# A two-layer attention decoder in split f32: four heads per attention unit on a fixed beat, the projection's last tiles by halves, residual loads for the MLP issued earlier

## The chip, the core and the metric

One core of one Trainium2 chip runs the whole program. The metric is the device time of one execution in microseconds (us). A core has a matrix engine (TensorE, PE in the tables; its loads of stationary operands are listed apart as PEld), VectorE (DVE), ScalarE (ACT), GpSimd (POOL) and SyncE (SP), which here only issues DMAs. Each engine runs its own instructions in order and waits on semaphores that the others raise.

## The reference

The kernel computes two layers of a decoder on a sequence of 1024 tokens with 1024 channels, all in f32:

```python
hn = rmsnorm(h, norm1[i])
# hn @ w_in: 256 pool columns, then q, k, v of 12 heads of 64
# 3 groups of 4 heads, (window, dilation) = (128,1), (512,4), (2048,16)
s = jnp.einsum('brnqhd,brnkhd->brnhqk', qs, kb) * (HEAD_DIM ** -0.5)
s = jnp.where(valid, s, -jnp.inf)
e = jnp.exp(s - jnp.max(s, axis=-1, keepdims=True))
o = jnp.einsum('brnqhk,brnkhd->brnqhd', e / l, vb)     # l: sum of e
# outputs of the three groups weighed by softmax of their log-sum-exps
h = h + concat(pool mixer, attention) @ w_out
# then rmsnorm, a squared-ReLU MLP of width 4096 and its residual add,
# then a gated per-layer embedding; after both layers a last rmsnorm
```

A block is 128 queries of one group. It sees one or two blocks of 128 keys.

## The kernel before

**How products are made.** An f32 operand is split into a high and a low part that the matrix engine takes at full speed (type fp32r), and a product is three matmuls: high by high, high by low, low by high. Activations lie transposed, 128 channels by 1024 tokens in a buffer. `products_by_row` (L570) makes several outputs at once, one row of the operand after another. The MLP's up and down products use a scheme of seven products per 2x2 block of tiles (class Seven): the pieces of a step are called P1 to P7 and run in the order P1, P7, P6, P2, P5, P4, P3, in groups of matmuls whose outputs are called X, Y and Z in the traces. For it, activations (`xP`, `wP`) and weights (`u0p`, `u1p` for up, `d0p`, `d1p` for down) are combined and split ahead: ScalarE writes the high part (L330 for weights), VectorE the low part (L332), GpSimd makes the weights' sums (`u0s`, L311 to L318).

**What sets the order.** The order of instructions is written by hand through a clock object `ck`. Each matmul of a large product advances it by a modelled time (`ck.tick(225.0)`), and generators that were started with `ck.go` are resumed when the modelled time that they asked for has come: their instructions then land between the large matmuls. `ck.need` and `ck.waiting` hold an instruction back until the one that writes its operand has been written down. So small matmuls of attention lie among the 128x512 matmuls of the input projection (`in` in the rows) and of the output projection (`po`).

**Buffers.** One SBUF pool has 49 buffers of equal size (`blk`). A buffer that the program drops is given to the next request, and its new writer waits until the last reader is through. PSUM banks come from four tags: `mm` (3 banks), `s` (2), `e` (2), `o` (1).

**Attention.** `attend` (L833) starts one generator `unit` (L763 to L831) per block and, in groups 0 and 1, per pair of heads, spaced by 3400 of modelled ns; group 2 has one unit for all four heads, every 2500. A unit writes down: the scores `s` (L783); per head a masked copy with the row maximum on VectorE (L789), a scaled maximum `nm` (L793), and the exponentials on ScalarE (L796); then the transposes `e` through the identity (L805), a copy of them to SBUF (`et`, L810 or L812), the products with v (`o`, L819) and the copies of these (L825, L828).

**End of the projection.** The output projection has eight tiles of 128 channels, each of two halves of 512 tokens. Tiles 0 to 5 go one half after another (L1122 to L1132). Tiles 6 and 7 are made together: four outputs in banks `mm`, `o`, `e`, `e`, interleaved by rows of the operand, and all four end with the last row:

```python
        outs = [(bank(f"po{L}", ("mm", "o", "e", "e")[k]), wk(ws[k % 2], range(8)), hs(k // 2)) for k in range(4)]
        products_by_row(outs, catl)
        ck.go(last_evac([o[0] for o in outs]))
```

`products_by_row` drops row i of the operand (`cat`, a high and a low buffer for each of the eight rows) when its products are written down. `last_evac` (L1070) then adds the residual to both halves (L1079 from PSUM, L1081) and starts the splits for the MLP (`xpiece`, L1040 to L1046); `combine` (L1094 to L1114) makes further pieces. The MLP's first group of matmuls (X, Y, Z, L566) follows at once.

**Residual in the MLP.** The residual was stored to memory as `h_d`. In the down products each piece's result is added to an accumulator `acc` (L1242), whose tiles are loaded from `h_d` (L1290) when piece P1 of a step is written down. SyncE also issues the loads of the activations' pieces (`wP` from `x_d`, L1226), their stores (L1199 to L1216) and the loads of weights (`d0r`, L284).

Of the kernel before, what the change touches and what calls it, by code (L numbers as in the profile page):

```python
# [9 lines left out]
F32 = mybir.dt.float32  # L10
# [106 lines left out]
def body(nc, tc, pools, A, out):  # L117
    sb, small, ps, dr = pools
    ck = Clock()
# [501 lines left out]
    def layer(L, hT, norm, tabs):  # L621
# [141 lines left out]
        def unit(g, n, ps_, q, k, vget, o, lag):  # L763

            two = (n > 0) if g == 0 else (n % 2 == 1) if g == 1 else False
            nb = 2 if two else 1
            np_ = len(ps_)
            K = 128 * nb
            if g == 2:
                mk = cst[:, C_MASK[2]:C_MASK[2] + 128]  # L770
            else:
                mk = cst[:, C_MASK[g] + 256 - K:C_MASK[g] + 256]
            heads = [(i, hh, 2 * p + hh) for i, p in enumerate(ps_) for hh in range(2)]
            for p in ps_:
                for t in (q[p], k[p]):
                    for hf in range(2):
                        ck.need((id(t), hf))
            sp = [bank(f"s{g}", "s", (128, np_, K)) for _ in range(2)]
            k0 = (n - nb + 1) * 128
            for i, hh, h in heads:  # L780
                r = slice(64 * hh, 64 * hh + 64)
                p = ps_[i]
                nc.tensor.matmul(sp[hh][:, i], q[p][r, n * 128:n * 128 + 128],  # L783
                                 k[p][r, k0:k0 + K], start=True, stop=True)
            ck.now += 218.0 * nb * np_
            yield 350.0
            sm = blk(f"sm{g}", F32, (128, np_, 2, K))
            for i, hh, h in heads:
                nc.vector.tensor_tensor_reduce(sm[:, i, hh], sp[hh][:, i], mk, 1.0, -3.0e38,  # L789
                                               OP.add, OP.max, ml[g][:, n, h:h + 1])  # L790
            nm = small.tile([128, 2 * np_], F32, name="nm", tag="nm", bufs=6)
            h0 = 2 * ps_[0]
            nc.vector.tensor_scalar(nm, ml[g][:, n, h0:h0 + 2 * np_], -0.125, None, op0=OP.mult)  # L793
            yield 500.0 + 300.0 * nb * np_
            for j, (i, hh, h) in enumerate(heads):
                nc.scalar.activation(sm[:, i, hh], sm[:, i, hh], AF.Exp, bias=nm[:, j:j + 1],  # L796
                                     scale=0.125, accum_out=ml[g][:, n, 4 + h:5 + h])
            yield 900.0 * np_ + 300.0
            if ps_[-1] == 1:
                stats_out(g, n)  # L800
            stats[g] += np_
            ep = bank(f"e{g}", "e", (128, np_, 2, nb, 128))
            for i, hh, h in heads:
                for kb in range(nb):
                    nc.tensor.transpose(ep[:, i, hh, kb], sm[:, i, hh, kb * 128:kb * 128 + 128], ident)  # L805
            ck.now += 107.0 * 2 * nb * np_
            yield 300.0
            et = blk(f"et{g}", F32, (128, np_, 2, nb, 128))
            if (n + ps_[0]) % 2:
                nc.vector.tensor_copy(et, ep)  # L810
            else:
                nc.scalar.activation(et, ep, AF.Copy)  # L812
            yield 900.0 + lag
            while not all(vok(g, n, p) for p in ps_):
                yield 500.0
            op = bank(f"o{g}", "o", (128, np_, 128))
            for i, hh, h in heads:
                for kb in range(nb):
                    nc.tensor.matmul(op[64 * hh:64 * hh + 64, i], vget(n - nb + 1 + kb, h),  # L819
                                     et[:, i, hh, kb], start=kb == 0, stop=kb == nb - 1)  # L820
            ck.now += 107.0 * 2 * nb * np_
            yield 300.0
            for i, p in enumerate(ps_):
                if g == 0:
                    nc.scalar.activation(o[p].rearrange("p (r n a) -> p n r a", r=8, n=8)[:, n],  # L825
                                         op[:, i].rearrange("p (r a) -> p r a", r=8), AF.Copy)
                elif g == 1:
                    nc.scalar.activation(o[p].rearrange("p (s x a) -> p x s a", s=2, x=8)[:, n],  # L828
                                         op[:, i].rearrange("p (s a) -> p s a", s=2), AF.Copy)
                else:  # L830
                    nc.scalar.activation(o[p][:, n * 128:n * 128 + 128], op[:, i], AF.Copy)  # L831

        def attend(g, q, k, vget, base, gap, lag=0.0):  # L833
            o = [blk(f"o{g}{p}_{L}") for p in range(2)]
            oT[g] = o
            i = 0
            for n in range(8):
                for ps_ in (((0, 1),) if g == 2 else ((0,), (1,))):
                    ck.go(unit(g, n, ps_, q, k, vget, o, lag), ("o", g, n, ps_[-1]), base + gap * i)
                    i += 1  # L840

        for g in range(2):
# [4 lines left out]
                   5000.0, 3400.0)  # L847
# [4 lines left out]
               3500.0, 2500.0)  # L852
# [121 lines left out]
        def weigh(g, p, hf):  # L974
            i = 2 * g + p
            keys = {("wb", g, p)}
            for n in range(4 * hf, 4 * hf + 4) if g == 2 else range(8):
                keys.add(("o", g, n, 1 if g == 2 else p))
# [91 lines left out]
        def last_evac(ps_):  # L1070
            add = nc.vector.tensor_tensor
            halves = []
            for k in (0, 1):
                res[6 + k] = blk(f"res{6 + k}_{L}")
            for hf in range(2):
                for m in (6, 7):
                    a = res[m][:, hs(hf)]
                    halves.append(a)
                    add(a, ps_[2 * hf + m - 6], f(hT[m][0][:, hs(hf)]), op=OP.add)  # L1079
                for m in (6, 7):  # L1080
                    add(res[m][:, hs(hf)], res[m][:, hs(hf)], f(hT[m][1][:, hs(hf)]), op=OP.add)  # L1081
                    P = {(6, 0): "P1", (7, 0): "P2", (7, 1): "P3"}.get((m, hf))
                    if P:
                        g = gt[:, G_N2 + 8 * L + m:G_N2 + 8 * L + m + 1]
                        ck.go(xpiece(3, P, res[m][:, hs(hf)], g, 2600.0 if P == "P3" else 900.0))
                yield 2800.0
# [4 lines left out]
            for k, a in enumerate(halves):  # L1091
                yield from norm2.add(a, k // 2)
# [440 lines left out]
```

## Time and profile before

| | us |
|---|---|
| median of 3 runs | 2332.04 (2331.57 to 2335.32) |
| the profiled execution, whole | 2332.01 |
| its span, first to last instruction | 2330.2 |
| PE busy | 2280.8 (98%) |
| DVE, ACT, POOL busy | 1677.5, 1014.7, 694.3 |

The rows below are of four kinds: the page's table of engines; the waits of one engine, added up by line and by what ended them; timelines, which list the instructions of an engine in a stretch with their start and their duration, and in brackets the idle time before them with what ended it; and a table of stretches with the granted clock. Layer 1 runs from the start to about 1150 us, layer 2 after it. Durations in a timeline overlap: a matmul's row reaches from its start to its modelled end, so what a matmul costs is read from one start to the next.

### The profile page before, as it was taken

What the parts mean: (1) busy time and instruction counts of PE and PEld (TensorE: products, weight loads), DVE (VectorE), ACT (ScalarE), POOL (GpSimd) and SP (SyncE); (2) the same over time, 40 slices, a digit from 0 to 9 for tenths busy, and PEclk for the clock granted to TensorE, in tenths of its full rate; (3) what the DMA queues carried; (4) which work ended last, traced back from release to release, by engine and by line L of the source; (5) the groups of instructions that cost most, each with busy time, mean ns of one, the idle gap of its engine ahead of it and who ended that gap; (6) DMA issues with size and microseconds to landing.
All of it is one profiled execution on the core that took longest, in us unless ns stands there. A gap on an engine that the chain in (4) does not pass through costs nothing.

```text
span 2330.2 us, 30901 instructions
## 1 busy us (share of the span) xinstructions
PE 2280.8 (98%) x11088; PEld 1841.8 (79%) x11088; DVE 1677.5 (72%) x2832; ACT 1014.7 (44%) x2147; POOL 694.3 (30%) x538
## 2 busy tenths in 40 slices
PE   8999999999999999999999999999999999999998
PEld 6767788788887788888887767878888877888888
DVE  7555677787778787886565467688777787787845
ACT  5243543433345444354324345434333443434645
POOL 5111136333332232342221122354333323333322
PEclk9999999999999999999999999999999999999999
DMA  5011133254447745432220111433444575545214
GB/s 181 19 38 28 38 92 109 77 171 153 155 150 257 234 136 164 148 95 70 61 59 19 38 38 39 106 112 117 155 156 157 198 237 179 172 127 169 89 55 136
DMA packets 296369, 275.65 MB, mean 118 GB/s; under 512 B 12476, under 2 KB 224056, under 8 KB 296216
## 3 DMA queue, kind: packets, MB, share of 16 engines
q1 hardware_dynamic: 293624, 270.04, 37.3%
q0 software_dynamic: 2272, 3.61, 0.9%
q8 instruction: 87, 1.43, 0.3%
q14 instruction: 66, 0.54, 0.1%
q10 hardware_dynamic: 320, 0.03, 0.0%
HBM read 200.99 MB, written 72.58 MB: 117 GB/s over the span
## 4 chain that ended last, share of the span: by engine, by line
PE 82%; DVE 8%; DMA 3%; POOL 2%; ACT 2%; issue 2%; SPq 0%; DVEq 0%; ACTq 0%; POOLq 0%
PE X L566 27%; PE Z L566 12%; PE Y L566 7%; PE in L551 6%; PE in L549 6%; PE in L553 5%; PE gt L553 2%; PE gt L551 2%; PE gt L549 2%; PE s L783 2%; PE o L819 2%; DVE wP L1230 2%; DMA wP<-x_d 2%; PE e L805 1%; POOL res L1058 1%
## 5 line engine op out<-in xcount | busy, mean ns | idle before, releaser
L1230 DVE TENSOR_TENSOR wP<-wP 128x512 fp32r<-128x512 f32 x252 | 197.5, 808 | 0.9 <-ACT wP L1228 0.9
L566 PE MATMUL X<-wP,d1p 128*128 128x512 f32 x768 | 186.2, 395 | 10.2 <-DVE acc L1242 9.7
L566 PE MATMUL X<-wP,d0p 128*128 128x512 f32 x768 | 186.2, 395 | 10.0 <-DVE acc L1242 9.5
L566 PE MATMUL X<-xP,u0p 128*128 128x512 f32 x768 | 183.2, 391 | 0.4 <-ACT y L1164 0.4
L566 PE MATMUL X<-xP,u1p 128*128 128x512 f32 x768 | 183.1, 391 | 0.4 <-ACT y L1164 0.4
L566 PEld LDWEIGHTS X<-wP,d0p 128*128 128x128 f32 x768 | 145.5, 191 | 44.4 <-DVE acc L1242 6.9
L566 PEld LDWEIGHTS X<-wP,d1p 128*128 128x128 f32 x768 | 145.4, 190 | 44.6 <-DVE acc L1242 7.2
L566 PEld LDWEIGHTS X<-xP,u0p 128*128 128x128 f32 x768 | 144.6, 189 | 30.9 <-ACT y L1164 0.8
L566 PEld LDWEIGHTS X<-xP,u1p 128*128 128x128 f32 x768 | 144.6, 189 | 30.9 <-ACT y L1164 0.8
L1190 ACT ACTIVATE y<-y 128x1024 f32<-128x1024 f32 x64 | 67.5, 1055 | 211.8 <-DVE y L1187 211.8
L1228 ACT ACTIVATE wP<-wP 128x512 fp32r<-128x512 f32 x252 | 147.3, 617 | 24.6 <-DMA wP<-x_d 22.2
L190 DVE SCALAR_TENSOR_TENSOR wl<-wr,gt,wh 128x128 fp32r<-128x128 f32 (+1 forms) x288 | 119.9, 447 | 38.5 <-ACT wh L196 38.3
L678 POOL TENSOR_TENSOR rot<-rot,s 128x512 f32<-128x512 f32 x48 | 61.4, 1284 | 278.6 <-DVE rot L676 217.6
L1242 DVE TENSOR_TENSOR acc<-acc,X 128x512 f32<-128x512 f32 x128 | 87.4, 683 | 77.9 <-PE X L566 63.8
L796 ACT ACTIVATE sm<-sm,nm 128x128 f32<-128x128 f32 (+1 forms) x192 | 84.5, 442 | 93.3 <-DVE nm L793 93.1
L196 ACT ACTIVATE wh<-wr,gt 128x128 fp32r<-128x128 f32 (+1 forms) x304 | 104.3, 396 | 0.5 <-DMA wr<-in_w_in_dram 0.5
L566 PE MATMUL Z<-xP,u0p 128*128 128x512 f32 x384 | 93.5, 393 | 4.6 <-DVE res L1079 4.6
L566 PE MATMUL Z<-xP,u1p 128*128 128x512 f32 x384 | 93.5, 393 | 4.5 <-DVE res L1079 4.5
L789 DVE CUSTOM_DVE_ANT_0 sm<-s,cst 128x128 f32<-128x128 f32 (+1 forms) x192 | 58.3, 347 | 52.1 <-PE s L783 52.0
L566 PE MATMUL Z<-wP,d0p 128*128 128x512 f32 x384 | 91.9, 389 | 0.0
L566 PE MATMUL Z<-wP,d1p 128*128 128x512 f32 x384 | 91.9, 389 | 0.0
L330 ACT ACTIVATE d0p<-d0s 128x512 fp32r<-128x512 f32 x64 | 40.1, 628 | 111.9 <-PE X L566 65.7
(474 smaller groups left out, 5923.8 us busy)
## 6 DMA issues: line engine op xcount, KB each, us to landing
wP<-x_d SPq DMA_DIRECT2D x252, 256.0 KB, 3.6
x_d<-ys SPq DMA_DIRECT2D x64, 512.0 KB, 3.6
wr<-in_w_in_dram SPq DMA_DIRECT2D x40, 512.0 KB, 4.2
u0r<-in_w_up_dram SPq DMA_DIRECT2D x32, 512.0 KB, 5.1
x_d<-y SPq DMA_DIRECT2D x32, 512.0 KB, 2.8
u1r<-in_w_up_dram SPq DMA_DIRECT2D x32, 512.0 KB, 5.4
d0r<-in_w_down_dram SPq DMA_DIRECT2D x28, 512.0 KB, 5.8
d1r<-in_w_down_dram SPq DMA_DIRECT2D x28, 512.0 KB, 5.9
```

What stands on the lines that cost most here:

```text
L190: nc.vector.scalar_tensor_tensor(l[:, k], raw[:, k], gs[k], f(h[:, k]), op0=OP.mult, op1=OP.subtract)
L196: nc.scalar.activation(h[:, k], raw[:, k], AF.Copy, scale=gs[k])
L549: nc.tensor.matmul(p, wh, h[:, cols], start=first and i == 0, stop=False)
L551: nc.tensor.matmul(p, wh, l[:, cols], start=False, stop=False)
L553: nc.tensor.matmul(p, wl, h[:, cols], start=False, stop=last and i == n - 1)
L566: nc.tensor.matmul(p, w[:, a, i], x[:, b], start=first and i == 0 and a == b == 0, stop=i == n - 1 and a == 1, skip_group_check=not first)
L678: nc.gpsimd.tensor_tensor(a, a, tb["s"][:, hs(hf)], op=OP.mult)
L796: nc.scalar.activation(sm[:, i, hh], sm[:, i, hh], AF.Exp, bias=nm[:, j:j + 1], scale=0.125, accum_out=ml[g][:, n, 4 + h:5 + h])
L1190: nc.scalar.activation(y, y, AF.Square)
L1228: nc.scalar.activation(t[:, 0], f(t[:, 1]), AF.Copy)
L1230: nc.vector.tensor_tensor(t[:, 1], f(t[:, 1]), f(t[:, 0]), op=OP.subtract)
L1242: nc.vector.tensor_tensor(a, a, p, op=OP.add)
```

## The change

Three parts. **Attention:** `unit` becomes a class `Unit` with all four heads of a block in every group. In groups 0 and 1 one generator `beats` writes down, every 5900 of modelled ns, the transposes of the block before, the products with v of the block before that and the scores of the current block, one behind another with no large matmul between. In group 2 the beat stays 2500 and the transposes come two beats after the scores. The four `nm` become one operation per block, and the copies of the transposes of a two-key-block unit are split over VectorE and ScalarE. **Projection:** tiles 6 and 7 are made for the first half of the tokens, in the two banks `e`, and then for the second half, in `mm` and `o`; `last_evac` is called after each; rows of `cat` are dropped in the second pass only. **Residual loads:** the tiles of step 0 are asked for five pieces ahead of the end of the up products, those of step k+1 at piece P4 of step k.

```diff
-    def products_by_row(outs, rhs, first=0, n=8):
+    def products_by_row(outs, rhs, n=8, last=True):
...
-            rhs[i] = None
+            if last:
+                rhs[i] = None
...
+            def beats():
+                t = ck.now
+                for i in range(8 + 2 * late):
+                    if 0 <= i - late < 8:
+                        u = units[i - late]
+                        u.turn()
+                        if g == 2:
+                            ck.go(alone(u))
+                    if g < 2 and i >= 2 * late:
+                        u = units[i - 2 * late]
+                        while not (vok(g, u.n, 0) and vok(g, u.n, 1)):
+                            yield 500.0
+                        u.mix()
+                    if i < 8:
+                        units[i].scores()
+                    t += gap
+                    yield max(100.0, t - ck.now)
...
             attend(g, q, k, lambda n, h, v=v: v[h // 2][:, n, 64 * (h % 2):64 * (h % 2) + 64],
-                   5000.0, 3400.0)
+                   5000.0, 5900.0, 1)
...
-               3500.0, 2500.0)
+               3500.0, 2500.0, 2)
...
-        outs = [(bank(f"po{L}", ("mm", "o", "e", "e")[k]), wk(ws[k % 2], range(8)), hs(k // 2)) for k in range(4)]
         cat.clear()
-        products_by_row(outs, catl)
-        ck.go(last_evac([o[0] for o in outs]))
+        for hf in range(2):
+            outs = [(bank(f"po{L}", ("e", ("mm", "o")[m])[hf]), wk(ws[m], range(8)), hs(hf)) for m in range(2)]
+            products_by_row(outs, catl, last=hf == 1)
+            ck.go(last_evac([o[0] for o in outs], hf))
...
+        def acc_load(t):
+            for m in (2 * t, 2 * t + 1):
+                acc[m] = blk(f"acc{m}_{L}")
+                nc.sync.dma_start(out=acc[m], in_=h_d[m])
...
+            if q == len(seq) - 5:
+                acc_load(0)
...
+            if P == "P4" and k < 3:
+                acc_load(k + 1)
             if P == "P1":
-                for m in (2 * t, 2 * t + 1):
-                    if acc[m] is None:
-                        acc[m] = blk(f"acc{m}_{L}")
-                        nc.sync.dma_start(out=acc[m], in_=h_d[m])
```

What this does to the order of instructions is shown at three places.

On the matrix engine, in group 0 of layer 1, among the input projection (`in`): `o` is the product with v, `s` the scores, `e` the transposes. Before:

```order
L819 MATMUL o0_1280<-et0_1266,v01_0_793 64x128 x4
L553 MATMUL in0_1203<-h0_5H_116,wl8_1017 128x512
L549 MATMUL in0_1203<-h0_6H_118,wh8_1016 128x512
L551 MATMUL in0_1203<-h0_6L_119,wh8_1016 128x512
L553 MATMUL in0_1203<-h0_6H_118,wl8_1017 128x512
L549 MATMUL in0_1203<-h0_7H_120,wh8_1016 128x512
L783 MATMUL s0_1295<-k01_0_553,q01_0_137 128x256
L783 MATMUL s0_1296<-k01_0_553,q01_0_137 128x256
L805 MATMUL e0_1299<-cst_68,sm0_1270 128x128 x4
L551 MATMUL in0_1203<-h0_7L_121,wh8_1016 128x512
```

and now:

```order
L551 MATMUL in0_1182<-h0_6L_119,wh8_1006 128x512
L816 MATMUL e0_1255<-cst_68,sm0_1223 128x128 x4
L816 MATMUL e0_1256<-cst_68,sm0_1223 128x128 x4
L835 MATMUL o0_1266<-et0_1190,v00_0_718 64x128 x4
L835 MATMUL o0_1266<-et0_1190,v01_0_793 64x128 x4
L784 MATMUL s0_1275<-k00_0_552,q00_0_136 128x256
L784 MATMUL s0_1276<-k00_0_552,q00_0_136 128x256
L784 MATMUL s0_1275<-k01_0_553,q01_0_137 128x256
L784 MATMUL s0_1276<-k01_0_553,q01_0_137 128x256
L553 MATMUL in0_1182<-h0_6H_118,wl8_1007 128x512
```

The small matmuls of four heads stand in one run between two large matmuls; before, two heads had theirs in two runs.

On ScalarE, at the end of the output projection (`xP` are pieces of the MLP's activations, `u0p` the high parts of its first weights; the semaphores that an instruction waits for stand in brackets). Before:

```order
L1040 ACTIVATE xP_3759<-t_0_3728 128x512 [waits DVE_49,PE_49]
L330 ACTIVATE u0p<-u0r_3701 128x512 [waits DMAHW5_49,DVE_49,Pool_49]
L330 ACTIVATE u0p<-u0r_3705 128x512 [waits DMAHW7_49,PE_49]
L330 ACTIVATE u0p<-u0r_3701 128x512 [waits PE_49]
L330 ACTIVATE u0p<-u0r_3705 128x512 [waits DVE_49,Pool_49]
L330 ACTIVATE u0p<-u0s_3756 128x512 [waits PE_49]
L330 ACTIVATE u0p<-u0s_3775 128x512 [waits PE_49]
L1044 ACTIVATE xP_3867<-res_0_3862,gt 128x512 [waits DVE_49,PE_49]
L1044 ACTIVATE xP_3870<-res_0_3863,gt 128x512 [waits DVE_49,PE_49]
```

and now:

```order
L1083 ACTIVATE xP_3635<-t_0_3604 128x512 [waits DVE_49,PE_49]
L1087 ACTIVATE xP_3674<-res_0_3669,gt 128x512 [waits DVE_49,PE_49]
L1087 ACTIVATE xP_3677<-res_0_3671,gt 128x512 [waits DVE_49,PE_49]
L330 ACTIVATE u0p<-u0r_3577 128x512 [waits DMAHW5_49,PE_49]
L330 ACTIVATE u0p<-u0r_3581 128x512 [waits DMAHW7_49,PE_49]
L330 ACTIVATE u0p<-u0r_3577 128x512 [waits PE_49]
L330 ACTIVATE u0p<-u0r_3581 128x512 [waits PE_49]
L330 ACTIVATE u0p<-u0s_3632 128x512 [waits PE_49,Pool_49]
L330 ACTIVATE u0p<-u0s_3651 128x512 [waits PE_49,Pool_49]
```

The splits of the last activations (L1044, now L1087) stood behind the first six splits of the weights and stand ahead of them now, and the weights' splits wait for the matrix engine in every row, since their buffers are those that the second pass drops.

On SyncE, around the second step of the down products. Before:

```order
L1226 DMA wP_6355<-x_d_3_3875 128x512
L284 DMA d0r_6391<-in_w_down_dram 128x8x128
L284 DMA d0r_6393<-in_w_down_dram 128x8x128
L1290 DMA acc_0_6430<-h_d_3209 128x1024
L1290 DMA acc_0_6432<-h_d_3209 128x1024
L1226 DMA wP_6451<-x_d_4_3876 128x512
```

and now:

```order
L1272 DMA wP_6233<-x_d_3_3761 128x512
L1285 DMA acc_0_6269<-h_d_3088 128x1024
L1285 DMA acc_0_6271<-h_d_3088 128x1024
L284 DMA d0r_6273<-in_w_down_dram 128x8x128
L284 DMA d0r_6275<-in_w_down_dram 128x8x128
```

The two loads of the residual stood behind the weights' loads and stand ahead of them now.

## Rows read from the trace of the kernel before

**Rows 1.** Waits of PE: who waited <- for whom: us in total, times, longest.

```profile
PE X L566 <- DVE acc L1242: 19.2, 14, 5.1
PE Z L566 <- DVE res L1079: 9.1, 2, 4.6
PE o L819 <- DVE et L810: 1.5, 2, 0.8
```

**Rows 2.** Stretches: us, PE busy (instructions), granted clock, DMA share, GB/s.

```profile
422.31:426.75 4.44, 4.44 (x11) 0.50 0.58 232
...
741.24:744.19 2.95, 2.95 (x7) 0.50 1.05 404
...
784.41:788.56 4.15, 4.15 (x11) 0.59 1.13 316
```

**Rows 3.** PE timeline (start us, us, line, operation), a run of `s` alone.

```profile
281.57 0.48 PE L553 MATMUL in<-h_1H,wl 128*128 128x512 f32 x1
281.98 0.71 PE L783 MATMUL s<-k,q 64*128 64x128 f32 x8
...
282.96 0.39 PE L551 MATMUL in<-h_2L,wh 128*128 128x512 f32 x1
283.19 0.40 PE L553 MATMUL in<-h_2H,wl 128*128 128x512 f32 x1
```

**Rows 4.** PE timeline, a run of `o` alone.

```profile
152.79 0.39 PE L553 MATMUL in<-h_5H,wl 128*128 128x512 f32 x1
153.11 0.66 PE L819 MATMUL o<-et,v 128*64 128x128 f32 x8
...
154.04 0.40 PE L551 MATMUL in<-h_6L,wh 128*128 128x512 f32 x1
```

**Rows 5.** PE timeline, `o` and `s` in one run.

```profile
266.31 0.39 PE L553 MATMUL in<-h_5H,wl 128*128 128x512 f32 x1
266.62 0.67 PE L819 MATMUL o<-et,v 128*64 128x128 f32 x8
267.22 0.71 PE L783 MATMUL s<-k,q 64*128 64x128 f32 x8
...
268.20 0.39 PE L551 MATMUL in<-h_6L,wh 128*128 128x512 f32 x1
```

**Rows 6.** Timeline of DVE and ACT, the softmax of one two-head unit.

```profile
151.85 0.42 DVE L789 CUSTOM_DVE_ANT_0 sm<-s,cst 128x256 f32<-128x256 f32 x1 [1.56 <-PE s L783]
...
152.20 0.42 DVE L789 CUSTOM_DVE_ANT_0 sm<-s,cst 128x256 f32<-128x256 f32 x1
...
152.67 0.17 DVE L793 TENSOR_SCALAR nm<-ml 128x2 f32<-128x2 f32 x1
...
152.93 0.51 ACT L796 ACTIVATE sm<-sm,nm 128x256 f32<-128x256 f32 x1 [0.76 <-DVE nm L793]
```

**Rows 7.** Timeline of DVE and POOL shortly before the projection's end.

```profile
399.05 0.68 DVE L1106 TENSOR_TENSOR t<-t 128x512 f32<-128x512 f32 x1
...
400.31 1.78 DVE L1042 TENSOR_TENSOR xP<-t,xP 128x512 fp32r<-128x512 f32 x1
...
405.36 1.29 POOL L311 TENSOR_TENSOR u0s<-u0r,u0r 128x512 f32<-128x512 f32 x1 [0.42 <-DMA u0r<-in_w_up_dram]
```

**Rows 8.** Timelines of DVE, SP (its DMA queue) and PE around residual loads; the last row is layer 2.

```profile
740.40 0.69 DVE L1242 TENSOR_TENSOR acc<-acc,X 128x512 f32<-128x512 f32 x1 [3.05 <-DMA acc<-h_d]
...
771.00 1.24 SPq L284 DMA_DIRECT2D d0r<-in_w_down_dram  x2
...
777.81 0.88 SPq L1290 DMA_DIRECT2D acc<-h_d x2
...
783.66 0.69 DVE L1242 TENSOR_TENSOR acc<-acc,X 128x512 f32<-128x512 f32 x1 [4.42 <-DMA acc<-h_d]
...
784.41 4.60 PE L566 MATMUL X<-wP,d0p 128*128 128x512 f32 x12 [3.20 <-DVE acc L1242]
...
1883.93 0.69 DVE L1242 TENSOR_TENSOR acc<-acc,X 128x512 f32<-128x512 f32 x1 [1.96 <-DMA acc<-h_d]
```

More of the change, by code (lines that the diff above doesn't have):

```diff
@@ L761, in stats_out @@
                 nc.gpsimd.dma_start(out=mlp[g], in_=st_d[g].rearrange("(t c) e -> c t e", c=128))
[L763 to L799, printed above, removed]
-                stats_out(g, n)
[L801 to L831, printed above, removed]
@@ L834, in attend, with alone @@
+        def attend(g, q, k, vget, base, gap, late):
             o = [blk(f"o{g}{p}_{L}") for p in range(2)]
             oT[g] = o
[L836 to L840, printed above, removed]
+            units = [Unit(g, n, q, k, vget, o) for n in range(8)]
+            def alone(u):
+                yield 1500.0
+                while not vok(g, u.n, 0):
+                    yield 500.0
[6 more added lines that the diff above has]
+                        u.turn()
+                        if g == 2:
+                            ck.go(alone(u))
+                    if g < 2 and i >= 2 * late:
+                        u = units[i - 2 * late]
+                        while not (vok(g, u.n, 0) and vok(g, u.n, 1)):
+                            yield 500.0
+                        u.mix()
+                    if i < 8:
+                        units[i].scores()
+                    t += gap
+                    yield max(100.0, t - ck.now)
+            ck.go(beats(), delay=base)
@@ L977, in weigh @@
             for n in range(4 * hf, 4 * hf + 4) if g == 2 else range(8):
-                keys.add(("o", g, n, 1 if g == 2 else p))
+                keys.add(("o", g, n, 1))
             while keys & ck.waiting:
@@ L1068, in out_evac, with last_evac @@
             yield from norm2.add(a, hf)
-        def last_evac(ps_):
+        halves = []
+        def last_evac(ps_, hf):
             add = nc.vector.tensor_tensor
[L1072 to L1086, printed above, removed]
+            for m in (6, 7):
+                if hf == 0:
+                    res[m] = blk(f"res{m}_{L}")
+                a = res[m][:, hs(hf)]
+                halves.append((a, hf))
+                add(a, ps_[m - 6], f(hT[m][0][:, hs(hf)]), op=OP.add)
+            for m in (6, 7):
+                add(res[m][:, hs(hf)], res[m][:, hs(hf)], f(hT[m][1][:, hs(hf)]), op=OP.add)
+                P = {(6, 0): "P1", (7, 0): "P2", (7, 1): "P3"}.get((m, hf))
+                if P:
+                    g = gt[:, G_N2 + 8 * L + m:G_N2 + 8 * L + m + 1]
+                    ck.go(xpiece(3, P, res[m][:, hs(hf)], g, 2600.0 if P == "P3" else 900.0))
+            if hf == 0:
+                return
+            yield 2800.0
             for m in (6, 7):
@@ L1090, in last_evac @@
             yield 6000.0
-            for k, a in enumerate(halves):
-                yield from norm2.add(a, k // 2)
+            for a, hf in halves:
+                yield from norm2.add(a, hf)
         def combine(i):
@@ L1132, in layer @@
         ws = [W.next(), W.next()]
[L1133 removed]
         cat.clear()
[L1135 to L1136 removed]
+        for hf in range(2):
+            outs = [(bank(f"po{L}", ("e", ("mm", "o")[m])[hf]), wk(ws[m], range(8)), hs(hf)) for m in range(2)]
+            products_by_row(outs, catl, last=hf == 1)
+            ck.go(last_evac([o[0] for o in outs], hf))
         outs = ws = w = None
```

79 lines of the change are left out of this document (78 added, 1 removed).

## The prediction

> **What bounds the kernel now.** I read the table of engines first: PE is busy 98% of the span, so a change can gain in two ways only, by taking idle time of PE away or by making the same matmuls cost less. The waits of PE come next [rows 1]. Two of them belong to places that the change touches: matmuls of group X that wait for VectorE's additions to the residual accumulator (19.2 us in 14 waits), and two that wait for the residual additions at the end of the projection (9.1 us, one in each layer). The table of stretches shows what such a wait costs behind itself [rows 2]: the granted clock is 0.50 for 4.44 us after the projection's wait, 0.50 for 2.95 us after one of the accumulator's, 0.59 over 4.15 us after the other (0.50 is 1.2 GHz, 1.00 is 2.4 GHz). Work that runs at half clock for t us loses t/2, so these are 2.2, 1.5 and 1.7 us, once in each layer. The third view is PE's timeline in the attention, where nothing is idle and something is lost all the same; that is the first part.
>
> **Attention: fewer runs of small matmuls.** The change issues the same matmuls, 10,558 in both orders by my count, so what moves is where they stand. A large matmul takes 0.23 us from start to start (282.96 to 283.19) [rows 3]. From the start of the large matmul ahead of a run to the start of the second one behind it, I subtract two of these, 0.46. A run of `o` alone then costs 154.04 − 152.79 − 0.46 = 0.79 us [rows 4], a run of `s` alone 282.96 − 281.57 − 0.46 = 0.93 [rows 3], and a run that has both 268.20 − 266.31 − 0.46 = 1.43 [rows 5]. One joint in place of two separate runs saves 0.79 + 0.93 − 1.43 = 0.29 us. In the two orders of PE I count runs of small matmuls with `s` or `o` in them, over both layers: 158 before, 72 now, so 86 joints, 86 × 0.29 = 24.9 us. Runs that hold only transposes or the like fall from 54 to 28. No pair of rows prices such a joint; it lies between 0 and the 0.29 of the others, 0 to 7.5 us for 26, and I take 0.08 each, 2.1 us, nearer to zero, since transposes use the array in the same shape as the large matmuls do and `s` and `o` do not (64*128 and 128*64 against 128*128 in the rows). The short waits of `o` for its copy (1.5 us) [rows 1] go too: a copy now has a whole beat. Sum: **28.5 us**. Below, it could be 18: the joints of `o` with `s` are priced by rows, those of transposes with `o` are not, and if about 24 of the 86 gain nothing, 62 × 0.29 = 18. Above, 112 × 0.29 + 1.5 = 34.
>
> What the rows leave open is what 0.29 pays for. If it is the change of the array's shape, the count to take is that of shape changes, 318 in the order before and 168 now, 150 fewer. The rule is in the Trainium skill, TensorEngine Tiling (Array Packing), section Tiling Modes, under Key Properties: a change of tiling mode drains the engine, a change of tile within the mode does not. The trace agrees in kind; by the rule with 0.29 for each change the gain would be 43.5 us, not 27. I keep the rows' count and carry this as a rival.
>
> **What the joints cost.** The softmax now has less time. In the order, 15 large matmuls stand between a block's scores and its transposes, 15 × 0.23 = 3.45 us, and PE waits if the exponentials are late. From the rows of a two-head unit [rows 6]: masked copies follow each other every 0.35 us (151.85 to 152.20), `nm` starts 0.82 after the first of two, the first exponential 0.26 after that, and each takes 0.51. With four heads: start 0.1 after the scores, `nm` at 0.1 + 0.82 + 2 × 0.35 = 1.62, exponentials done at 2.39, 2.90, 3.41 and 3.92. They are needed at 3.45 and then about every 0.2 us (two transposes each), the fourth at about 4.05. So it fits, with as little as 0.15 us for the last head, and other work of ScalarE and VectorE may come between. I take no cost; each 0.1 us by which it is late is 3.2 us over the 32 beats (8 blocks, 2 groups, 2 layers).
>
> **Residual loads.** The first accumulator wait: VectorE was idle 3.05 us until the load came and then added [rows 8]. In SyncE's order the load now stands ahead of seven loads of `wP` that it stood behind. It holds them up by its own issue, 0.9 us for such a pair [rows 8], and its transfer; their users, the splits of the pieces, come several loads later. VectorE is busy up to the start of these 3.05 us, so that is what goes, and about 2 us of the wait of 5.1 [rows 1] stay. In layer 2 the idle time is 1.96 [rows 8]. Together 5.0 us. The second: the load was issued at 777.81, the addition ran at 783.66, 5.85 us behind it, and PE had waited 3.20 [rows 8]. In the order it now stands ahead of two weight loads that were issued at 771.00 [rows 8], 6.8 us earlier; with the same way to landing it is there at about 776.9, before VectorE's idle time of 4.42 us begins, and the wait goes, 3.2 in each layer (I take layer 2 alike), 6.4. No wait, no fall of the clock: 2 × 1.7 = 3.4 more [rows 2]. After the first wait 2 us of idle time remain, and whether the clock falls then no row shows: 0 to 3.0 us for both layers, I take half, 1.5. Sum: **16.3 us**, between 11 (if the loads land only half as much earlier at the second place, and the clock falls) and 18.
>
> **Projection by halves.** Meant to go is the wait of 4.55 us in each layer (9.1 in two) [rows 1] and the 2.2 us behind it: the bank that Z waits for is now emptied while the second half is still being made. The order shows what comes in its place. The 16 buffers of `cat` are dropped in the second pass, not in the only one, and the next writers take them: VectorE's last piece of the step before, ScalarE's high parts of the first weights, GpSimd's sums, all of them wait for PE in the second pass now. The pass takes 48 × 0.23 = 11 us. Call its end E. VectorE's chain starts at about E − 9.8, when the row whose buffer it takes is through. It has five operations, four additions and two splits of the new half, and then six low parts of weights. GpSimd's eight sums, 1.3 us each at the least, fall into the same time, and beside them an operation of VectorE with both inputs in SBUF took 1.78 us where one took 0.68 without [rows 7]. With 1.78 for these, ScalarE's first high part, which now stands behind the splits of the last activations, is there at about E + 3.4, VectorE's first low part at E + 6.4. PE would wait about 6.0 us at E in two pieces (3.4, then 2.6 more for the low parts) in place of 4.55, with the same fall of the clock: a loss of 1.4 in each layer, **−2.9 us**. With 0.68 for all of them everything is there before E, nothing is waited for, and it is a gain of 2 × (4.55 + 2.2) = 13.5 us. At the other end, with one more slow operation per layer ahead of the low parts, −6. I take the slow price, since GpSimd's sums are held to the same stretch by the same buffers.
>
> Here a rule bears on the price. In the trace a slow operation lasts 1.78 us, a quick one 0.68 and one of GpSimd's sums 1.29 [rows 7]. The Trainium skill, SBUF — State Buffer, section Who interferes with whom, states that a VectorE instruction with two SBUF inputs contends with a GpSimd instruction that reads SBUF, one blocking the other for a whole instruction. The trace agrees that such a pair is slow; taking turns would give 0.68 + 1.29 = 1.97 for a pair, and with six such the sum above would be −5 us, not −2.9.
>
> **Sum.** 28.5 + 16.3 − 2.9 = 41.9 us. The profiled execution took 2332.01 in all, 0.03 below the median, so the same sum holds for both: 2332 − 42 = **2290 us**.
>
> **Rivals.** (1) The halves work as meant: GpSimd's sums or VectorE's chain are through before E. For it: the sums are spread over 13 us, not all of them meet a VectorE operation. Against: the buffers' waits in the order. It gives 2290 − 2.9 − 13.5 = 2274. (2) Each change of shape costs 0.29: 16.5 us more, 2274. Against it: two changes would take 0.58 of the 0.79 of a run of eight `o`, which leaves 26 ns for each matmul. (3) The softmax is late by about 0.5 us in each of 32 beats: −16, 2306. For it: the slack of 0.15 us, and ScalarE has the copies of `et` and `o` in the same stretch. (4) The residual loads gain little: both waits stay half as long, the clock falls as before. For it: a DMA share above 1.0 in these stretches [rows 2], so that an earlier load can be a longer one, and the buffers that it waits for. It gives 2332 − 28.5 − 5.7 + 2.9 = 2301. (5) Slower than before: the same mechanism as in (3), with the transposes late by more than 41.9 / 32 = 1.3 us in each beat, because another operation of ScalarE or VectorE stands ahead of the exponentials in most of them. At 2 us it is 64 lost against 42 gained, 2354. Against it: between the scores and the transposes the order has one or two other operations of 0.3 to 0.6 us in a beat, not four.
>
> **Chances.** The forecast 0.44, (1) 0.20, (2) 0.09, (3) 0.12, (4) 0.11, (5) 0.04. The bounds of the forecast's terms reach from 2332 − 34 − 18 + 2.9 = 2283 to 2332 − 18 − 11 + 6 = 2309; (1) and (2) reach to 2274 and a little below where their terms add up. I take 2271 to 2310, which leaves out (5), the worse half of (3) and both of (1) and (2) together. About 0.2%, 4.7 us, is what a measurement of this kernel can tell from no change. Slower by more than that is (5), 0.04; within it are mixtures of (3) and (5), 0.03; faster is the rest, 0.93.
>
> **What would show it.** In the profile after: the same matmuls with PE busy some 25 us less; no wait, or small ones, of transposes for the exponentials, and where they are, rival (3); the wait for the accumulator 19.2 us down to about 8; no fall of the clock near 785 us; in place of Z waiting for the residual, X or Z of the first up group waiting for low parts of `u0p`, about 6 us in each layer, with a fall of the clock behind it. I am wrong in the mechanism if the busy time of PE does not fall while the waits do, or if the first up group starts without a wait.

## The result, and the profile after

| | before | after |
|---|---|---|
| median | 2332.31 (2331.57 to 2335.32, 4 runs) | 2303.47 (2300.31 to 2305.06, 4 runs) |
| span of the profiled execution | 2330.2 | 2302.2 |
| PE busy | 2280.8 | 2256.9 |

The ratio is 0.9866, 95% interval 0.9854 to 0.9878. The kernel is 28.8 us faster, where 42 were forecast; 2303.5 lies within the range of 2271 to 2310. The kernel before was timed again beside each experiment and took 2334.2 to 2335.4 us there, 2 to 3 us more than here, so kernels are compared below by their ratio to it (0.9866 for the change) or by stretches of their traces, not by their times alone. Which term fell short is read by cutting both executions at the same places of the program, the first product of the input projection, the end of the output projection, the first and last of the down products. Before, layer 1 (us from the start, length, PE busy with instructions, granted clock, DMA share, GB/s):

```profile
10.00:414.87 404.87, 401.61 (x2169) 1.00 0.24 67
414.87:730.10 315.23, 310.26 (x1369) 0.99 0.47 152
730.10:1050.80 320.70, 310.69 (x1346) 0.99 0.54 169
```

and after:

```profile
10.20:401.20 391.00, 388.36 (x2168) 1.00 0.25 69
401.20:718.40 317.20, 311.20 (x1370) 0.99 0.48 155
718.40:1037.90 319.50, 311.83 (x1346) 0.98 0.53 166
```

Layer 2, cut in the same way, goes from 394.4, 315.2 and 320.7 to 380.6, 316.8 and 317.7. So over both layers the attention and the projection won 13.9 + 13.8 = 27.7 us (forecast 28.5), the up products, where the projection's halves show, lost 2.0 + 1.6 = 3.6 (forecast 2.9), and the down products, where the residual loads show, won 1.2 + 3.0 = 4.2, where 16.3 were forecast. Of the miss of 13 us, 12 lie in the third term.

The waits of PE after, which answer to [rows 1] (who waited <- for whom, us in total, times, longest):

```profile
PE X L566 <- DVE acc L1293: 13.3, 13, 3.0
...
PE X L566 <- DVE u1p L332: 3.0, 1, 3.0
PE X L566 <- DVE u0p L332: 3.0, 1, 3.0
PE X L566 <- ACT u0p L330: 2.5, 1, 2.5
PE X L566 <- ACT u1p L330: 2.5, 1, 2.5
```

The waits of Z for the residual (9.1 us) are gone, and four waits for the first up weights (11.0) stand in their place; the waits for the accumulator fell from 19.2 to 13.3. No wait of transposes for exponentials is in the list.

### The profile page after: what moved, and what is told of

It is laid out like the page before. It is cut to its first block, busy times and chain, and to the rows that moved or that the text cites. A ratio compares the mean times of both kernels' runs of the same rounds, so it can differ in the third digit from the quotient of the medians.

```text
span 2302.2 us, 30845 instructions
## 1 busy us (share of the span) xinstructions
PE 2256.9 (98%) x11088; PEld 1856.8 (81%) x11088; DVE 1660.0 (72%) x2790; ACT 1014.3 (44%) x2147; POOL 696.8 (30%) x538
## 3 DMA queue, kind: packets, MB, share of 16 engines
q8 instruction: 87, 1.43, 0.3%
## 4 chain that ended last, share of the span: by engine, by line
PE 84%; DVE 8%; DMA 3%; ACT 2%; issue 2%; POOL 0%; SPq 0%; DVEq 0%; ACTq 0%
PE X L566 26%; PE Z L566 12%; PE Y L566 6%; PE in L551 5%; PE in L553 5%; PE in L549 5%; DMA wP<-x_d 3%; PE gt L553 3%; PE gt L549 3%; PE gt L551 3%; DVE wP L1276 2%; PE po L551 2%; PE po L549 2%; PE po L553 2%; PE o L835 2%
## 5 line engine op out<-in xcount | busy, mean ns | idle before, releaser
L1276 DVE TENSOR_TENSOR wP<-wP 128x512 fp32r<-128x512 f32 x252 | 203.0, 830 | 7.2 <-ACT wP L1274 7.2
L330 ACT ACTIVATE d1p<-d1s 128x512 fp32r<-128x512 f32 x64 | 40.3, 629 | 113.8 <-PE X L566 68.1
```

The costliest lines, as they stand in the source:

```text
L330: nc.scalar.activation(t[:, 0], src, AF.Copy)
L1276: nc.vector.tensor_tensor(t[:, 1], f(t[:, 1]), f(t[:, 0]), op=OP.subtract)
```

## Experiments on the attention

**The attention alone.** The changed kernel with the projection's last tiles and the residual loads put back as they were before:

```diff
-            if q == len(seq) - 5:
-                acc_load(0)
...
+            if P == "P1":
+                for m in (2 * t, 2 * t + 1):
+                    if acc[m] is None: ...
...
+        outs = [(bank(f"po{L}", ("mm", "o", "e", "e")[k]), wk(ws[k % 2], range(8)), hs(k // 2)) for k in range(4)]
+        products_by_row(outs, catl)
```

> Attention part alone, projection and residual loads as before. Theory (the parts add up, and the attention is worth what the stretch from the first input product to the last output product lost between the two traces, 13.8 us a layer): 2332.3 - 27.6 = 2304.7 us, PE busy about 27 us below before. Rival (part of that came from earlier residual loads or from the projection's halves): over 2312.

Measured 2307.3 us against 2334.7 for the kernel before beside it, ratio 0.9881 (0.9866 to 0.9896): 27.3 us. By the ratios the other two parts together win some 3.5 us more, and the intervals overlap; by the spans, 2302.1 here and 2302.2 for the changed kernel, they win nothing. The attention is nearly the whole gain, and the other two parts about cancel.

**What the joints are worth.** Two kernels separate "entering and leaving a run of small matmuls" from "changing the array's shape". In the first the transposes of a beat stand in a run of their own:

```diff
                         if g == 2:
                             ck.go(alone(u))
+                        else:
+                            yield 500.0
```

> The changed kernel with the transposes of a beat in a run of their own, a few large matmuls ahead of the run of o and s: 32 more runs, the same 168 changes of the array's shape. If entering and leaving a run is what costs: 32 x 0.29 = 9 us more, 2313. If the change of shape is what costs: 0 to 3 us more (0.08 each), 2304 to 2306.

In the second, half of the scores stand ahead of the products with v and half behind them:

```diff
-                        u.mix()
-                    if i < 8:
-                        units[i].scores()
+                        if i < 8:
+                            units[i].scores(u.mix)
...
+                    if first is not None and (p, hh) == (0, 1):
+                        first()
```

> The changed kernel with two of the four score products of a head pair ahead of the products with v and the others behind them, in the same run: 24 more changes of the array's shape, no more runs. If the change of shape is what costs: 24 x 0.17 to 0.29 = 4 to 7 us more, 2307.5 to 2310.5. If entering and leaving a run is what costs: 2303.5.

A beat of the changed kernel, PE timeline (start us, us, line, operation):

```profile
142.12 0.39 PE L551 MATMUL in<-h_0L,wh 128*128 128x512 f32 x1
142.35 1.03 PE L816 MATMUL e<-cst,sm 128*128 128x128 f32 x8
143.31 1.15 PE L835 MATMUL o<-et,v 128*64 128x128 f32 x16
144.39 1.13 PE L784 MATMUL s<-k,q 64*128 64x256 f32 x8
...
145.79 0.40 PE L549 MATMUL in<-h_1H,wh 128*128 128x512 f32 x1
```

The beat costs 145.79 − 142.12 − 0.46 = 3.21 us. The same with the scores split (second kernel):

```profile
143.17 0.39 PE L551 MATMUL in<-h_0L,wh 128*128 128x512 f32 x1
...
144.36 0.70 PE L784 MATMUL s<-k,q 64*128 64x256 f32 x4
145.00 1.14 PE L837 MATMUL o<-et,v 128*64 128x128 f32 x16
146.07 0.70 PE L784 MATMUL s<-k,q 64*128 64x256 f32 x4
...
147.04 0.40 PE L549 MATMUL in<-h_1H,wh 128*128 128x512 f32 x1
```

147.04 − 143.17 − 0.46 = 3.41 us: one more change of shape, 0.20 us. The span grew from 2302.2 to 2306.4 for 24 of these, 0.175 each; the two stretches of the attention alone grew by 2.6 and 2.4 us, 0.21 each (median 2307.1; the ratio 0.9881, 0.9866 to 0.9896, is not clear of that of the changed kernel by itself, the rows are). The first kernel, a run of transposes that waits for nothing, a run of `o` and `s`, and one where it waits:

```profile
107.70 0.39 PE L549 MATMUL in<-h_6H,wh 128*128 128x512 f32 x1
107.93 1.03 PE L816 MATMUL e<-cst,sm 128*128 128x128 f32 x8
...
109.03 0.39 PE L553 MATMUL in<-h_6H,wl 128*128 128x512 f32 x1
...
132.09 0.40 PE L551 MATMUL in<-h_7L,wh 128*128 128x512 f32 x1
132.42 1.15 PE L835 MATMUL o<-et,v 128*64 128x128 f32 x16
133.49 1.13 PE L784 MATMUL s<-k,q 64*128 64x256 f32 x8
...
134.89 0.39 PE L549 MATMUL in<-h_0H,wh 128*128 128x512 f32 x1
...
138.73 1.92 PE L816 MATMUL e<-cst,sm 128*128 128x128 f32 x8 [1.15 <-ACT sm L803]
```

The eight transposes cost 109.03 − 107.70 − 0.46 = 0.87 and the rest 134.89 − 132.09 − 0.46 = 2.34, together 3.21, to the hundredth what the joined beat costs. A joint without a change of shape is worth nothing. Of my two prices the shape's is the right one, at 0.17 to 0.21 us for a change.

The whole kernel took 2317.3 us all the same, 13.7 us of span more, which neither expectation had. The last row shows why: in that beat of layer 1 twelve large matmuls stand between the scores and the next transposes (134.56 to 138.73) in place of the changed kernel's fifteen or sixteen, and the exponentials are late. That is rival (3), the late softmax, made by an experiment: with 0.7 us less of cover this run of transposes cost 3.07 us (137.19 to 140.72, less 0.46) in place of 0.87. Added up in the same way, the runs of group 0 in this layer cost 6.6 us more than in the changed kernel, of the 7.7 us that its attention took longer. In the changed kernel the cover is enough: no such wait is in its list.

## Experiments on the projection's halves

**One pass as before**, attention and residual loads as changed:

```diff
-        for hf in range(2):
-            outs = [(bank(f"po{L}", ("e", ("mm", "o")[m])[hf]), wk(ws[m], range(8)), hs(hf)) for m in range(2)]
-            products_by_row(outs, catl, last=hf == 1)
-            ck.go(last_evac([o[0] for o in outs], hf))
+        outs = [(bank(f"po{L}", ("mm", "o", "e", "e")[k]), wk(ws[k % 2], range(8)), hs(k // 2)) for k in range(4)]
+        products_by_row(outs, catl)
+        ck.go(last_evac([o[0] for o in outs]))
```

> The changed kernel with the projection's last tiles in one pass as before. Theory (dropping cat's buffers late costs more than the early bank saves, 1.9 and 1.6 us in the two layers): 2303.5 - 3.5 = 2300 us, and the wait of Z for the residual of 4.5 us with half clock behind it is back, while no wait for u0p is left. Rival (the halves work as meant and something else lost the time): 2303.5 or more.

Measured 2299.5 us, ratio 0.9852 (0.9837 to 0.9867), span 2299.7 against 2302.2. The wait of Z is back (9.1 us in two), none for `u0p` is left. The halves are a loss of 2.5 us by the spans and 3.4 us in the two stretches of the up products; the ratios' intervals overlap.

**Why the first weights are late.** In the changed kernel, VectorE, ScalarE and PE around the projection's end, which is at 401.2 (called E as in the prediction), and one of GpSimd's eight sums, which fill 393.3 to 406.9 (start us, us, operation, in brackets the idle time before it and what ended it):

```profile
391.65 0.75 DVE L1153 SCALAR_TENSOR_TENSOR t<-res,gt,t 128x512 f32<-128x512 f32 x1 [1.08 <-PE po L577]
...
393.28 1.72 POOL L311 TENSOR_TENSOR u0s<-u0r,u0r 128x512 f32<-128x512 f32 x1 [6.34 <-PE po L577]
393.77 1.78 DVE L1157 SCALAR_TENSOR_TENSOR t<-res,gt,t 128x512 f32<-128x512 f32 x1
395.48 3.48 DVE L1085 TENSOR_TENSOR xP<-t,xP 128x512 fp32r<-128x512 f32 x2
...
402.36 3.44 DVE L1089 SCALAR_TENSOR_TENSOR xP<-res,gt,xP 128x512 fp32r<-128x512 f32 x2
403.16 2.17 ACT L330 ACTIVATE u0p<-u0r 128x512 fp32r<-128x512 f32 x4
403.83 0.73 PE L566 MATMUL X<-xP,u0p 128*128 128x512 f32 x2 [2.47 <-ACT u0p L330]
405.72 3.55 DVE L332 TENSOR_TENSOR u0p<-u0r,u0p 128x512 fp32r<-128x512 f32 x4
...
407.52 2.08 PE L566 MATMUL X<-xP,u0p 128*128 128x512 f32 x4 [2.96 <-DVE u0p L332]
```

VectorE waits for a buffer of the second pass until E − 9.6, seven of its operations then take 1.7 to 1.8 us each, and PE waits 2.47 + 2.96 = 5.43 us in two pieces. To see whether the late buffers or the slow operations do it, GpSimd's sums of the first two up steps were replaced by zeros, written by GpSimd into the same buffers at the same places:

```diff
+            if self.name[0] == "u" and j < 2:
+                add = lambda o, a, b, op: nc.gpsimd.memset(o, 0.0)
```

> The changed kernel with GpSimd's sums of the first two up steps left out: it writes zeros into the same buffers at the same places, so buffers and waits stay and GpSimd reads nothing from SBUF there. Theory (VectorE's operations with two SBUF inputs are slow beside GpSimd's sums, 1.78 for 0.68 us, and that makes the first up weights late): some seven of them 1.1 us shorter, the two waits at the first up group (2.5 and 3.0 us in each layer) nearly gone and the half clock behind them too: 2303.5 - 14 = 2289 us or a little above. Rival (the late release of cat's buffers is enough by itself): the waits stay, 2301 to 2303.

Measured 2287.5 us, ratio 0.9795 (0.978 to 0.9809). VectorE and PE in that kernel:

```profile
393.26 0.75 DVE L1159 SCALAR_TENSOR_TENSOR t<-res,gt,t 128x512 f32<-128x512 f32 x1
...
398.11 1.42 DVE L1091 SCALAR_TENSOR_TENSOR xP<-res,gt,xP 128x512 fp32r<-128x512 f32 x2 [0.25 <-ACT xP L1089]
399.44 2.49 DVE L334 TENSOR_TENSOR u0p<-u0r,u0p 128x512 fp32r<-128x512 f32 x4
...
400.69 1.52 PE L568 MATMUL X<-xP,u0p 128*128 128x512 f32 x6
```

The same operations take 0.6 to 0.75 us each, the low parts come 6.3 us earlier (5.8 counted from the projection's end), and the first up group starts without a wait. With the buffers as late as before, the wait goes when GpSimd no longer reads SBUF beside VectorE's operations with two inputs from there. The rule that the prediction weighed, VectorE and GpSimd contending for such reads (the Trainium skill, SBUF — State Buffer, Who interferes with whom), is borne out by this pair of kernels; that writes alone do not contend is also what it states, and the zeros that GpSimd wrote slowed nothing here.

**Twelve of sixteen buffers early.** Rows 0 to 5 of the operand in one pass, 6 and 7 by halves:

```diff
+        outs = [(bank(f"po{L}", ("e", "e", "mm", "o")[k]), wk(ws[k % 2], range(8)), hs(k // 2)) for k in range(4)]
+        products_by_row(outs, catl, n=6)
         for hf in range(2):
-            outs = ...
-            products_by_row(outs, catl, last=hf == 1)
-            ck.go(last_evac([o[0] for o in outs], hf))
+            products_by_row(outs[2 * hf:2 * hf + 2], catl, first=6, last=hf == 1)
+            ck.go(last_evac([o[0] for o in outs[2 * hf:2 * hf + 2]], hf))
```

> The changed kernel with the projection's last tiles made in one pass for rows 0 to 5 of the operand, dropped as they go, and by halves for rows 6 and 7 alone; first half in the banks e. Theory (the early bank is worth 6 us a layer, and only the late release of 16 buffers spoils it): twelve of the 16 buffers come free as before, no wait at the first up group, 2303.5 - 16 = 2288 us. Rival (additions of the first half still too late behind the weights' low parts, or these behind GpSimd): a wait of 2 to 4 us stays in each layer, 2295 to 2300.

Measured 2301.9 us, ratio 0.9858 (0.9843 to 0.9872), above the 2288 expected and above the rival's 2295 to 2300. The wait at the first up group did fall, to 0.92 us, though GpSimd's sums are still there: two of VectorE's low parts beside them still take 3.47 us together, but earlier. So the wait needs both, the late buffers and the slow operations, and all but goes when either is taken away. Another wait came 14 us later in its place (PE and ScalarE of this kernel):

```profile
419.06 0.63 ACT L1083 ACTIVATE xP<-t 128x512 fp32r<-128x512 f32 x1 [1.67 <-POOL sq_b L457]
419.60 1.13 ACT L455 ACTIVATE sqt_b<-res 128x512 f32<-128x512 f32 x2
...
422.19 1.06 ACT L1211 ACTIVATE y<-X 128x512 f32<-128x512 f32 x2
422.82 2.50 PE L566 MATMUL X<-xP,u0p 128*128 128x512 f32 x5 [4.32 <-ACT y L1211]
```

PE now needs the bank of the first up result early, and ScalarE, which copies it out, has the squares of the last residual tiles for the norm ahead of that copy, in a queue that waits for GpSimd (`sq_b`). So these squares were asked for later, together with the residual loads of the next section:

```diff
-            yield 6000.0
+            yield 12000.0
             for a, hf in halves:
                 yield from norm2.add(a, hf)
```

> Rows 0 to 5 in one pass and rows 6, 7 by halves (as in the run before), residual loads of step k+1 at piece P7, and the squares of the last residual tiles for the norm asked for 6000 of modelled ns later, so that ScalarE copies the first up results ahead of them. Theory (the wait of 4.3 us for ScalarE's copy that took the place of the first one comes from these squares, which wait for GpSimd): both waits of the up products nearly gone, 2303.5 - 13 - 7 = 2283 us. Rival (ScalarE is late by the chain of splits itself): the wait of about 4 us and its half clock stay, 2294.

Measured 2288.3 us, ratio 0.9804 (0.979 to 0.9818). The wait for the copy fell from 4.32 to 2.25 us, about half, since two squares still stand ahead of the copy, so neither expectation was met in full: 5 us above the one, 6 below the other. This kernel beats both before and after. The whole tiles in one pass, with the first half of the tokens in the banks `e` and the second in `mm` and `o`, and else the same as the last (which the text below calls the first kernel):

> As the first kernel of this call, but the projection's last tiles wholly in one pass, with the first half of the tokens in the banks e and the second in mm and o (before, the other way round). Theory (Z waits for a bank that VectorE empties only behind the weights' low parts, 3.4 us earlier for the first half than for the second): the wait of 4.5 us falls to about 1 us, no wait for u0p, 2284 to 2287. Rival (the banks are not what Z waits for): 2293.

Measured 2290.1 us, ratio 0.9809 (0.9795 to 0.9823), midway between the two expectations. PE's Z waits 0.49 us for the residual, where it waits 4.56 in the kernel with one pass, the old banks and the loads at P7 (the last of the next section); PE's wait for the copy is 1.8. Both the banks and the place of the squares differ between these two kernels, but VectorE's operations up to Z are the same (the first addition at 403.54 and 403.41) and the squares come behind it, so Z's wait is the banks' doing. Exchanging the banks takes nearly all of the wait that the halves were made for, without holding any buffer longer. In time the two are 0.9809 and 0.9828, with intervals that overlap.

## Experiments on the residual loads

In the changed kernel the second place of [rows 8] reads so (SyncE's queue, ScalarE, VectorE, PE):

```profile
757.39 0.93 SPq L1285 DMA_DIRECT2D acc<-h_d  x2
...
764.06 3.48 SPq L1272 DMA_DIRECT2D wP<-x_d  x6
...
769.38 1.23 ACT L1274 ACTIVATE wP<-wP 128x512 fp32r<-128x512 f32 x2 [7.54 <-DMA wP<-x_d]
770.04 2.40 DVE L1276 TENSOR_TENSOR wP<-wP 128x512 fp32r<-128x512 f32 x2 [3.27 <-ACT wP L1274]
...
775.26 0.67 DVE L1293 TENSOR_TENSOR acc<-acc,X 128x512 f32<-128x512 f32 x1
775.99 5.49 PE L566 MATMUL X<-wP,d0p 128*128 128x512 f32 x12 [3.00 <-DVE acc L1293]
```

VectorE no longer waits for a residual load anywhere in this stretch. But the loads of `wP` behind them landed so late that ScalarE waited 7.54 us for them and VectorE 3.27 for ScalarE, and the addition that frees PE's bank stands behind these splits in VectorE's order. PE waits two groups of matmuls later than before, 3.00 us in place of 3.20. To tell the loads' traffic from VectorE's order, one kernel leaves the residual out and sets the accumulators to zero with GpSimd in place of loading them (eight tiles of 512 KB, 4 MB a layer, not the 2 MB of the text below):

```diff
-                nc.sync.dma_start(out=acc[m], in_=h_d[m])
+                nc.gpsimd.memset(acc[m], 0.0)
```

> The changed kernel without the residual in the MLP: the accumulators are set to zero by GpSimd at the places where the loads were issued, so 2 MB a layer are not loaded and SyncE's queue is free of them. Theory (the residual loads stand ahead of loads of wP in a stretch where the DMA engines are full, and the late wP is what PE waits for now): the second wait of each layer (3.0 and 2.8 us) and the half clock behind it go, about 10 us: 2293. Rival (VectorE's order alone makes the wait): 2300 to 2303.

and one keeps the loads and issues them four pieces earlier (P7, P6, P2, P5, then P4):

```diff
-            if P == "P4" and k < 3:
+            if P == "P7" and k < 3:
                 acc_load(k + 1)
```

> The changed kernel with the residual loads of step k+1 at piece P7 of step k, four groups of matmuls (11 us) earlier, in a stretch where the DMA engines are busy by 0.1 to 0.6. Theory (what counts is what the loads collide with): the second wait of each layer goes, 2293 to 2297. Rival (buffers or the queue hold the wP loads up as much): 2303.

Measured 2298.5 us (ratio 0.9837, 0.9822 to 0.9852) and 2296.9 us (0.9833, 0.9817 to 0.985). The row of PE's second wait, without the loads and with the loads at P7:

```profile
774.35 3.03 PE L566 MATMUL X<-wP,d0p 128*128 128x512 f32 x12 [1.28 <-DVE acc L1293]
```

```profile
772.41 2.79 PE L566 MATMUL X<-wP,d0p 128*128 128x512 f32 x11 [1.28 <-DVE acc L1293]
```

Both give 1.28 us in layer 1: with the loads out of the way of `wP`, 1.7 of the 3.0 us go, and the rest is there even with no load at all. By the traces, what holds the rest is VectorE: in both kernels it has no idle time from 752 until the addition that frees the bank, and four of its operations there are slow beside GpSimd's sums of the down weights, two of them in this row (loads at P7):

```profile
764.86 1.74 POOL L313 TENSOR_TENSOR d0s<-d0r 128x512 f32<-128x512 f32 x1
765.36 3.49 DVE L1276 TENSOR_TENSOR wP<-wP 128x512 fp32r<-128x512 f32 x2
```

Such a pair takes 1.28 elsewhere in the same stretch, so this row alone is longer by 2.2 us than it need be; a kernel without these sums was not run. Layer 2 is less clean. PE's second wait there is 2.77 us in the changed kernel, 1.28 with the loads at P7, but 2.01 with no loads, since ScalarE still waited 6.08 us for `wP` in that kernel (7.12 in the changed one). So the residual loads are not the only thing that makes `wP` late; what else does was not tried. The theory took all of the wait for the loads' doing and was right for somewhat more than half of it in layer 1. In the down products of the kernel with P7 both layers took 315.4 us (716.9 to 1032.3, 1842.9 to 2158.3), 6.5 less than the changed kernel's 319.5 and 317.7 together. The earlier place with the projection in one pass as before was run too:

> The attention's part and residual loads at P7, projection in one pass as before. If the parts add up: 2299.5 - 6.6 = 2293 us. If the earlier residual loads collide with something that the projection's halves had delayed: 2299.

Measured 2293.4 us, ratio 0.9828 (0.9813 to 0.9842), as the sum of the parts says.

## Why the prediction was right in its range and 13 us off

**Attention, 28.5 forecast, 27.7 measured.** The size was right and the unit was not. I priced a joint at 0.29 us from [rows 3 to 5] and multiplied by 86. The run of `s` alone that I took in [rows 3] lies directly behind a matmul that follows a run of transposes (from 281.57 to 281.98 it takes 0.41, where the one ahead of another such run, 269.80 to 270.12, takes 0.32), so its 0.93 contains about 0.09 that belongs to that run; that other run of eight `s` costs 0.85, and 0.79 + 0.85 − 1.43 is 0.21. What is paid is 0.17 to 0.21 us for each change of the array's shape, and 150 changes fewer give 25.5 to 31.5 us. (The pages count 11,088 matmuls in each of the two kernels, not 10,558; that they are the same in both is what the sum needs.) The two counts agree here because three joints in a block of two key blocks take away five changes (3 × 0.29 = 0.87, 5 × 0.17 = 0.85; measured 4.04 − 3.21 = 0.83, with 2 × (0.79 + 1.23) before). Rival (2) had the mechanism and the wrong price, for the same reason.

**What the joints cost: nothing, as forecast.** No wait of transposes is in PE's list. How near the edge it is, the kernel with the transposes apart shows: with 0.7 us less of cover they are late. The slack of 0.15 us itself was not measured.

**Residual loads, 16.3 forecast, 4.2 measured.** The step that failed is "it is there before VectorE's idle time begins, and the wait goes, 6.4". The load was there; the wait stayed, turned over in the main to the loads of `wP` that I had let be pushed back for nothing, and the rest of it to VectorE, which stood full behind the loads and which I had not looked at. Rival (4) had the outcome, a small gain with the clock falling as before, but not this reason: it had the moved load itself take longer, or wait for its buffers. Of the first wait my step held: 5.09 and 5.08 fell to 3.03 and 1.96 in the two layers, 5.2 together for 5.0 forecast (in layer 1 one split ahead of the addition took 1.75 us). Of the second 0.5 us went in place of 6.4. The two make 5.7, and 4.2 were won, so some 1.5 us more than before went to half clock, where 4.9 were to come back (PE was busy 1.1 and 0.3 us longer with the same matmuls in the two stretches): behind every one of these four waits the clock still fell (columns as in the first table; behind the second wait of layer 1, and behind the first of layer 2, which lasted 1.96 us):

```profile
776.00:780.00 4.00, 4.00 (x10) 0.50 0.46 116
...
1856.63:1859.60 2.97, 2.97 (x8) 0.58 1.06 407
```

**Projection, −2.9 forecast, −3.6 measured.** By its own steps: PE starts at E + 2.6 with the first high part (3.4 forecast), goes on with the first low part at E + 6.3 (6.4), 5.4 us of waits (6.0). The slow price was the right choice: without GpSimd's reads the wait is gone, and, as the kernel with only rows 6 and 7 by halves shows, it is nearly gone as well (0.92 us) when twelve of the buffers come early. Rival (1) needed GpSimd's sums to miss VectorE's chain, and they met it.

## What to carry to other kernels

Small matmuls that use another shape of the array are best sorted by shape: in this kernel the change of shape was paid, 0.17 to 0.21 us, and the run was not; and a row that prices a change should have undisturbed neighbours on both sides. When a load is moved ahead in a full queue, the wait can go to what it overtakes, as it did here: name the user of that, and the instructions that stand behind the user, before booking the gain. Holding buffers longer cost here because their next writers then ran beside an engine that slowed them, so look first for an exchange of banks that frees the one that is waited for and holds nothing.

## What was not expected of the hardware

Two idle times of PE of nearly the same length, 1.95 and 1.96 us, at the same place of layer 1 and layer 2 of one execution (the kernel with the loads at P7), had different ends: the granted clock stayed at full in the one and was at half for most of the next 4 us in the other (length, PE busy with matmuls, clock, DMA share, GB/s).

```profile
724.90:728.90 4.00, 4.00 (x18) 1.00 1.05 412
...
1850.87:1854.87 4.00, 4.00 (x11) 0.57 1.05 415
```

So the length of an idle time of that size does not decide by itself. Other kernels say the same: behind 2.99 us (attention alone, to 1901.50) the clock stayed at full for the next 4 us, behind 1.78 us (exchanged banks, to 1891.41) it was 0.62 over them. What else decides, no run here tells.

Nor is half clock always lost time. In the kernel with the loads at P7 the down products took 315.4 us in both layers. Where the clock stayed at full, PE waited for VectorE again two groups on, 1.68 us; where it fell, that wait was 0.57. The prediction's price for a fall, 1.5 to 1.7 us each, would be paid in full only where PE does not wait for another engine soon after.
